# Moving six of nine group-norm tiles out of the end of a bidirectional recurrence into its last chunks

## The chip, the cores and the metric

The kernel runs on one core of one Trainium2 chip. The metric is the device time of one execution in microseconds. Its engines are TensorE (PE; weight loads are listed apart as PEld), VectorE (DVE), ScalarE (ACT), GpSimd (POOL) and SyncE (SP, which only issues DMAs here). ACT and POOL have DMA queues of their own.

## The reference, cut to what matters

The model has two layers of a first block and then a second block. Each layer of the first block projects 1040 tokens (16 meta tokens and 1024 real ones), runs a linear recurrence over the tokens in both directions, runs an attention (MLA) over the same tokens, mixes the two results with an output matrix, and goes through a mixture of experts. This case touches what follows the recurrence, the group norm of its output:

```python
y = y_f + y_b                       # forward and backward scan, (L, 8 heads, 64)
mu = jnp.mean(y, -1, keepdims=True)
var = jnp.mean(jnp.square(y - mu), -1, keepdims=True)
yn = ((y - mu) * lax.rsqrt(var + RWKV_GN_EPS)).reshape(B, L, RW) * gn_g + gn_b
out = (yn + (bonus_f + bonus_b).reshape(B, L, RW)) * g
```

It is elementwise over a row of 512 values, apart from one mean and one variance in each group of 64.

## The kernel before, in words

`recur` runs the scan in 17 chunks: chunk 0 holds the meta tokens forward, chunk c the 64 tokens from 16 + 64(c-1); the backward direction runs the same 17 chunks from the end. Both directions share each instruction, in the two halves of the 128 partitions. For chunk c the steps stand in the code in this order: `state` (PE products with the carried state S, then an ACT copy `Rs`), `solve` (PE product with an inverse `t64`, two ACT copies into `uv`), `next` (PE `dS`, then one DVE operation that updates S, L968), `out` (PE `Yp`, an ACT copy `ys`, two stores to `d_y` from POOL's queue, L978 and L981), and `bkt` for the chunk that follows (PE transposes and two ACT copies, L858).

The inverses are made ahead, for four chunks at a time, by `r_inv`: a DVE transpose, 31 pairs of small DVE multiplications and additions (`tm`, L876, and `Tn`, L877), and two more transposes (`TF`, `TT`). `turn` deals them out between the chunk's steps by a planned time: 2.2 us ahead of the S update, 0.8 us behind it, 5.2 us at the chunk's end, and all that is left at the end of every fourth chunk. `r_solve` turns `TT` into the `t64` of the next four chunks (copies on ACT, L893, and on POOL, L894, then PE and ACT). `r_prep`, which makes the DVE's masked products, looks eight chunks ahead, so chunks from 9 on have none of it.

`tc.manual_schedule` fixes the order of PE, ACT, DVE and SP in the loop to that of the code; each engine works its list in order. POOL's order, and everything behind the loop, is put in order by a planner at build time.

`r_post` does the group norm for one tile of up to 128 rows, nine tiles a layer, all called behind the loop. Its tiles come from a pool with two buffers, so a third tile waits for the first one's rows to be stored. A tile needs both directions of its rows, so tile 4 (rows 400 to 527) is complete after chunk 9, then 5, 3, 6, 2, 7, 1 one chunk apart, and 8 and 0 after chunk 16.

Behind `recur` in the code comes `mla`, which doesn't need the group norms; its weights are split into two parts by ACT and DVE (`split`, L251 and L252), then PE makes the products, and per block of tokens PE scores, a DVE maximum (L1151), ACT exponentials (L1155), PE transposes, and ACT and DVE copies and splits (L1166, L1169, L1170). The group norms' rows are first read in `mix_out`, behind the attention.

Of the kernel before, what the change touches and what calls it, by code (L numbers as in the profile page):

```python
# [10 lines left out]
F32 = mybir.dt.float32  # L11
# [5 lines left out]
ALU = mybir.AluOpType  # L17
# [155 lines left out]
class K:  # L173
# [521 lines left out]
    def recur(self, li, S):  # L695
        nc, tc, I = self.nc, self.tc, self.I
        with ExitStack() as es:
            LAG, GRP, N = 8, 4, 17

            def pool(name, bufs, **k):  # L700
                return es.enter_context(self.tpool(name=name, bufs=bufs, **k))

            ep = pool("r_e", 1)
            R = dict(li=li, S=S)
            R["dc"] = ep.tile([128, 32, 32], F32, name="dc")
            R["mask"] = []
            for d in range(2):
                m = ep.tile([128, 128], F32, name=f"cmask{d}")
                nc.sync.dma_start(m, self.C[f"cmask{d}"])
                R["mask"].append(m)  # L710
            bp, cp, mp = pool("r_b", 1), pool("r_c", 1), pool("r_m", 18)

            ap = pool("r_ar", 3)
            R.update(ap=ap, bp=bp, mp=mp, st=pool("r_s", 2), tp=pool("r_t", 2), qp=pool("q_t", 2, side="right"),
                     psa=pool("r_psa", 2, space=PSUM), psr=pool("r_psr", 2, space=PSUM),
                     psq=pool("r_psq", 2, space=PSUM), psc=pool("r_psc", 2, space=PSUM))
            R["t64"] = [cp.tile([128, 8 * GRP, 64], F32, name=f"t64{i}") for i in range(2)]
            for t in R["t64"] + [R["dc"]]:
                nc.gpsimd.memset(t, 0.0)

            R["pend"] = cp.tile([128, 8, N], F32, name="pend2")
            for d in range(2):
                for h in range(2):
                    nc.sync.dma_start(R["pend"][64 * d:64 * d + 64].rearrange("p (f h) c -> p f h c", h=2)[:, :, h],
                                      S["pend"][64 * h:64 * h + 64, d])
            R["St"] = [cp.tile([128, RW], F32, name=f"S{i}") for i in range(2)]
            qc = pool("q_c", 1, side="right")
            R["gb"] = self.bcast(qc, I["rwkv_gn_g"][li], RW, "gn_g")
            R["bb"] = self.bcast(qc, I["rwkv_gn_b"][li], RW, "gn_b")
            A = {}  # L730
            ET = mybir.EngineType
            with tc.manual_schedule(engines={ET.PE, ET.Activation, ET.DVE, ET.SP}):
                def turn(inv, left, us):

                    left += us
                    while left > 0:
                        w = next(inv, None)
                        if w is None:
                            return 0.0
                        left -= w  # L740
                    return left

                for s in range(GRP):
                    A[s] = self.r_prep(R, s)
                    for half in A[s]["halves"]:
                        half()
                    A[s]["diag"]()
                inv = self.r_inv(R, [A[c] for c in range(GRP)], 0)
                left = turn(inv, 0.0, 2.0)
                for s in range(GRP, LAG):  # L750
                    A[s] = self.r_prep(R, s)
                    if s == GRP:
                        V = self.r_load(R, 0)
                    for half in A[s]["halves"]:
                        half()
                        left = turn(inv, left, 3.5)
                    A[s]["diag"]()
                V["bkt"]()
                left = turn(inv, 0.0, 99.0)
                late = self.r_solve(R, [A[c] for c in range(GRP)], 0)  # L760
                next(late), next(late)
                C = self.r_chain(R, 0, A[0], V)
                C["own"]()
                for c in range(N):
                    g = c // GRP + 1
                    hs = [A[x] for x in range(GRP * g, min(N, GRP * g + GRP))]
                    if c % GRP == 0:
                        inv = self.r_inv(R, hs, g) if hs else iter(())
                        left = turn(inv, 0.0, 0.5)
                    P = None  # L770
                    if c + LAG < N:
                        P = A[c + LAG] = self.r_prep(R, c + LAG)
                    Vn = self.r_load(R, c + 1) if c + 1 < N else None
                    C["state"]()
                    next(late, None)
                    C["solve"]()
                    if P:
                        P["halves"][0]()
                    left = turn(inv, left, 2.2)
                    C["keep"]()  # L780
                    if Vn:
                        Cn = self.r_chain(R, c + 1, A[c + 1], Vn)
                        Cn["own"]()
                    C["next"]()
                    left = turn(inv, left, 0.8)
                    if P:
                        P["halves"][1]()
                    C["out"]()
                    next(late, None)
                    if P:  # L790
                        P["diag"]()
                    left = turn(inv, left, 99.0 if c % GRP == GRP - 1 else 5.2)
                    if Vn:
                        Vn["bkt"]()
                    if c % GRP == GRP - 1 and hs:
                        late = self.r_solve(R, hs, g)
                        next(late)
                    del A[c]
                    if Vn:
                        C = Cn  # L800
            for i in range(9):
                self.r_post(R, i)

    def r_fetch(self, pool, names, S, ch):

# [179 lines left out]
    def r_post(self, R, i):  # L985

        nc, tp, S, li = self.nc, R["qp"], R["S"], R["li"]
        gb, bb = R["gb"], R["bb"]
        c0, n = TT[i]
        y0 = tp.tile([128, RW], F32, name="q_y0")  # L990
        y1 = tp.tile([128, RW], F32, name="q_y1")
        v = tp.tile([128, RW], F32, name="q_v")
        g = tp.tile([128, RW], F32, name="q_g")
        for t, src in ((y0, S["y"][0]), (y1, S["y"][1]), (v, S["v"][0]), (g, S["g"])):
            (nc.gpsimd if t in (y0, y1) else nc.sync).dma_start(t[:n], src[c0:c0 + n, :])
        nc.gpsimd.tensor_tensor(y0[:n], y0[:n], y1[:n], ALU.add)
        yv = y0[:n].rearrange("p (h v) -> p h v", h=8)
        y1v = y1[:n].rearrange("p (h v) -> p h v", h=8)
        vv = v[:n].rearrange("p (h v) -> p h v", h=8)
        mu = tp.tile([128, 8], F32, name="q_mu")  # L1000
        nc.vector.tensor_reduce(mu[:n], yv, AX.X, ALU.add)
        nc.vector.tensor_scalar(mu[:n], mu[:n], 1.0 / 64, None, ALU.mult)
        nc.gpsimd.tensor_tensor(yv, yv, mu[:n, :, None].to_broadcast([n, 8, 64]), ALU.subtract)
        nc.scalar.activation(y1[:n], y0[:n], AF.Square)
        vr = tp.tile([128, 8], F32, name="q_vr")
        nc.vector.tensor_reduce(vr[:n], y1v, AX.X, ALU.add)
        nc.scalar.activation(vr[:n], vr[:n], AF.Sqrt, scale=1.0 / 64, bias=self.eps["gn"][:n])
        nc.vector.reciprocal(vr[:n], vr[:n])
        nc.gpsimd.tensor_tensor(vv, vv, S["bonus"][:n, i, :, None].to_broadcast([n, 8, 64]), ALU.mult)
        nc.gpsimd.tensor_tensor(v[:n], v[:n], bb[:n], ALU.add)  # L1010
        nc.vector.tensor_tensor(yv, yv, vr[:n, :, None].to_broadcast([n, 8, 64]), ALU.mult)
        nc.vector.tensor_tensor(y0[:n], y0[:n], gb[:n], ALU.mult)
        nc.vector.tensor_tensor(y0[:n], y0[:n], v[:n], ALU.add)
        nc.gpsimd.tensor_tensor(y0[:n], y0[:n], g[:n], ALU.mult)
        nc.scalar.dma_start(S["yr"][c0:c0 + n, :], y0[:n])
        if self.dbg:
            self.dbg(f"yr{li}", (T, RW), y0[:n], lambda a: a[c0:c0 + n])

# [1504 lines left out]
```

## Time and profile before

| | |
|---|---|
| three runs | 4386.04, 4390.46, 4396.25 us, median 4390.46 |
| the profiled execution | 4402.54 us, span 4400.7 us |
| busy share of the span | PE 87%, PEld 72%, DVE 63%, ACT 42%, POOL 22% |
| layer 1: last seven S updates to the end of its recurrence | 618.86 us to 679.04 us |
| layer 1: attention | 679.04 us to about 992 us |
| the same in layer 2 | 2187.08 us to 2247.75 us, and on to about 2551 us |

All times in a trace count from the start of the span. The busy share is an average over stages that have different limits: in the recurrence PE, ACT and DVE hand work to each other chunk by chunk, in the attention PE has most of the work. So what the change moves is read from the two stretches that it touches, once in each layer.

### The profile page before, as it was taken

How to read it: one execution, taken by the hardware profiler on the slowest of the kernel's cores; microseconds unless marked ns; L12 is line 12 of the kernel's file. 1: busy time of each engine (PE TensorE's matmuls, PEld its weight loads, DVE VectorE, ACT ScalarE, POOL GpSimd, SP SyncE). 2: the span in 40 equal slices, each digit the busy share in tenths (PEclk: the TensorE clock that was granted, in tenths of full speed). 3: DMA queues.
4: the chain of work that ended last, by engine and by line, in shares of the span. 5: the costliest groups of instructions: out<-in, count | busy, mean ns of one | idle time of the engine just before them, and what ended most of it. 6: DMA issues, size and time to landing. Idle time of an engine off the chain costs nothing. (4 is left out here: it accounts for less than half of the span.)

```text
span 4400.7 us, 68329 instructions
## 1 busy us (share of the span) xinstructions
PE 3830.7 (87%) x27155; PEld 3157.1 (72%) x27155; DVE 2767.7 (63%) x4684; ACT 1869.7 (42%) x3033; POOL 988.2 (22%) x719
## 2 busy tenths in 40 slices
PE   7888897899699688897887896997898889999998
PEld 7677676786576476776776775765786677888786
DVE  7763777757698757627668577997644753333354
ACT  4323445542387543233555532876424522111232
POOL 2331124201242243311233012331422410000000
PEclk9788798999799887886988997999998899999999
DMA  4446663113499833447641043998521121111232
GB/s 154 101 129 183 160 161 108 37 54 128 160 345 346 300 102 101 115 143 172 165 125 58 1 172 131 340 335 309 181 73 29 53 97 58 48 48 43 90 126 81
DMA packets 384153, 611.94 MB, mean 139 GB/s; under 512 B 50467, under 2 KB 217602, under 8 KB 381762
## 3 DMA queue, kind: packets, MB, share of 16 engines
q1 hardware_dynamic: 278402, 485.38, 35.3%
q10 hardware_dynamic: 85200, 70.97, 5.4%
q0 software_dynamic: 20224, 51.15, 3.7%
q8 instruction: 216, 3.54, 0.3%
q14 instruction: 111, 0.91, 0.1%
HBM read 491.65 MB, written 123.45 MB: 140 GB/s over the span
## 5 line engine op out<-in xcount | busy, mean ns | idle before, releaser
L252 DVE TENSOR_TENSOR w13l<-xw,w13h 128x1024 fp32r<-128x1024 f32 x248 | 296.4, 1220 | 57.5 <-ACT w13h L251 53.9
L251 ACT ACTIVATE w13h<-xw 128x1024 fp32r<-128x1024 f32 x256 | 267.4, 1058 | 130.3 <-PE x_hp L258 76.6
L256 PE MATMUL pp_ps<-T_hi,pw_hi 128*128 128x348 f32 x912 | 309.7, 340 | 8.7 <-ACT T_hi L1752 2.9
L257 PE MATMUL pp_ps<-T_lo,pw_hi 128*128 128x348 f32 x912 | 305.4, 335 | 1.4 <-DVE T_lo L1757 1.3
L258 PE MATMUL pp_ps<-T_hi,pw_lo 128*128 128x348 f32 x912 | 304.3, 334 | 0.0
L2414 PE MATMUL f_mm<-F_hi,f_wh 128*128 128x512 f32 x704 | 222.8, 398 | 1.7 <-ACT F_hi L251 1.7
L2414 PE MATMUL f_mm<-F_lo,f_wh 128*128 128x512 f32 x704 | 222.6, 397 | 0.0
L2414 PE MATMUL f_mm<-F_hi,f_wl 128*128 128x512 f32 x704 | 222.3, 397 | 0.0
L256 PE MATMUL x_hp<-w13h,x_h 128*96 128x512 f32 x512 | 208.5, 407 | 0.1
L257 PE MATMUL x_hp<-w13l,x_h 128*96 128x512 f32 x512 | 204.7, 400 | 0.0
L258 PE MATMUL x_hp<-w13h,x_l 128*96 128x512 f32 x512 | 204.0, 398 | 0.0
L256 PEld LDWEIGHTS pp_ps<-T_hi,pw_hi 128*128 128x128 f32 x912 | 179.8, 197 | 21.8 <-issue 7.8
L257 PEld LDWEIGHTS pp_ps<-T_lo,pw_hi 128*128 128x128 f32 x912 | 179.8, 197 | 5.1 <-DVE T_lo L1757 2.6
L287 POOL TENSOR_TENSOR g_x<-g_x,g2g 128x1024 f32<-128x1024 f32 x6 | 14.3, 2385 | 750.4 <-ACT g_x L284 750.4
L258 PEld LDWEIGHTS pp_ps<-T_hi,pw_lo 128*128 128x128 f32 x912 | 179.5, 197 | 3.0 <-issue 3.0
L252 DVE TENSOR_TENSOR f_wl<-F_raw,f_wh 128x1024 fp32r<-128x1024 f32 x44 | 53.7, 1221 | 203.2 <-ACT f_wh L251 203.2
L251 ACT ACTIVATE f_wh<-F_raw 128x1024 fp32r<-128x1024 f32 x44 | 46.4, 1060 | 307.0 <-PE f_mm L2414 301.4
L1616 POOL DMA_INDIRECT d_y<-x_o,r_idx x64 | 102.8, 1606 | 312.1 <-DVE x_al L252 288.8
L825 PE MATMUL aa<-ar_p,bk_p 64*128 64x128 f32 x1088 | 134.0, 376 | 40.2 <-DVE A L827 33.6
L2414 PEld LDWEIGHTS f_mm<-F_hi,f_wh 128*128 128x128 f32 x704 | 133.1, 189 | 34.4 <-ACT F_hi L251 2.0
L2414 PEld LDWEIGHTS f_mm<-F_lo,f_wh 128*128 128x128 f32 x704 | 132.7, 189 | 32.8 <-DVE F_lo L252 0.6
L2414 PEld LDWEIGHTS f_mm<-F_hi,f_wl 128*128 128x128 f32 x704 | 132.9, 189 | 32.4
(630 smaller groups left out, 11221.3 us busy)
## 6 DMA issues: line engine op xcount, KB each, us to landing
xw<-in_moe_w SPq DMA_DIRECT2D x256, 512.0 KB
xw<-in_moe_w SPq DMA_DIRECT2D x64, 1024.0 KB
wd_raw<-in_w_down SPq DMA_DIRECT2D x44, 512.0 KB
pw_raw<-in_w_in SPq DMA_DIRECT2D x36, 512.0 KB
d_AR<-AR ACTq DMA_DIRECT2D x32, 544.0 KB
d_BK<-BK ACTq DMA_DIRECT2D x32, 544.0 KB
ar_p<-d_AR SPq DMA_DIRECT2D x68, 256.0 KB
bk_p<-d_BK SPq DMA_DIRECT2D x68, 256.0 KB
```

The source lines that it names most:

```text
L251: nc.scalar.activation(hi, src, AF.Copy)
L252: (lo_eng or nc.vector).tensor_tensor(lo, src, hi.bitcast(F32), ALU.subtract)
L256: mm(out, wh, xh, start=first, stop=False)
L257: mm(out, wh, xl, start=False, stop=False)
L258: mm(out, wl, xh, start=False, stop=last)
L287: e1.tensor_tensor(out[:n], out[:n], gb[:n], ALU.mult)
L825: nc.tensor.matmul(aa[d][:, h - z], bk[q, h], ar[q, h], start=True, stop=True)
L1616: nc.gpsimd.indirect_dma_start(out=y2[:, :], out_offset=bass.IndirectOffsetOnAxis(ap=si, axis=0), in_=y, in_offset=None, bounds_check=2 * ...
L2414: nc.tensor.matmul(p[:, j], a[:, k], b[:, k, 512 * j:512 * j + 512], start=st, stop=sp)
```

## The change

`r_post` becomes a generator with four steps, and six of the nine tiles (4, 5, 3, 6, 2, 7) are started in chunks 10 to 15, one a chunk, behind `out`. Every half chunk each open tile is taken one step on: `norms` is called behind `out`, and behind the last `turn` ahead of the next chunk's `bkt`. The steps are: (1) the loads (y0 and y1 from POOL's queue, v and g from SP's) and two POOL operations on v; (2) the sum of both directions, now on DVE where it was on POOL, the sum over the group and its scaling on DVE, and the subtraction on POOL; (3) the square on ACT and its sum on DVE; (4) the root on ACT, and the rest. The finished rows are stored from POOL's queue where it was ACT's. Tiles 1, 8 and 0 run behind the loop as before, in that order.

```diff
+                order, rows = [4, 5, 3, 6, 2, 7, 1, 8, 0], []
+                rest = [self.r_post(R, i) for i in order]
+
+                def norms(c, new=False):
+                    if new and 10 <= c < 16:
+                        rows.append(rest.pop(0))
+                    for r in list(rows):
+                        if next(r, 0) == 0:
+                            rows.remove(r)
                 for c in range(N):
...
                     C["out"]()
+                    norms(c, True)
                     next(late, None)
                     if P:
                         P["diag"]()
                     left = turn(inv, left, 99.0 if c % GRP == GRP - 1 else 5.2)
+                    norms(c)
                     if Vn:
                         Vn["bkt"]()
...
-            for i in range(9):
-                self.r_post(R, i)
+            for r in rows + rest:
+                for _ in r:
+                    pass
...
-        nc.gpsimd.tensor_tensor(y0[:n], y0[:n], y1[:n], ALU.add)
...
+        vr = tp.tile([128, 8], F32, name="q_vr")
+        nc.gpsimd.tensor_tensor(vv, vv, S["bonus"][:n, i, :, None].to_broadcast([n, 8, 64]), ALU.mult)
+        nc.gpsimd.tensor_tensor(v[:n], v[:n], bb[:n], ALU.add)
+        yield
+        nc.vector.tensor_tensor(y0[:n], y0[:n], y1[:n], ALU.add)
         nc.vector.tensor_reduce(mu[:n], yv, AX.X, ALU.add)
         nc.vector.tensor_scalar(mu[:n], mu[:n], 1.0 / 64, None, ALU.mult)
         nc.gpsimd.tensor_tensor(yv, yv, mu[:n, :, None].to_broadcast([n, 8, 64]), ALU.subtract)
+        yield
         nc.scalar.activation(y1[:n], y0[:n], AF.Square)
-        vr = tp.tile([128, 8], F32, name="q_vr")
         nc.vector.tensor_reduce(vr[:n], y1v, AX.X, ALU.add)
+        yield
         nc.scalar.activation(vr[:n], vr[:n], AF.Sqrt, scale=1.0 / 64, bias=self.eps["gn"][:n])
         nc.vector.reciprocal(vr[:n], vr[:n])
-        nc.gpsimd.tensor_tensor(vv, vv, S["bonus"][:n, i, :, None].to_broadcast([n, 8, 64]), ALU.mult)
-        nc.gpsimd.tensor_tensor(v[:n], v[:n], bb[:n], ALU.add)
...
         nc.gpsimd.tensor_tensor(y0[:n], y0[:n], g[:n], ALU.mult)
-        nc.scalar.dma_start(S["yr"][c0:c0 + n, :], y0[:n])
+        nc.gpsimd.dma_start(S["yr"][c0:c0 + n, :], y0[:n])
```

## Rows read from the trace of the kernel before

**Rows 1.** Attention by windows: us, busy us of each engine (instructions), PE clock, DMA share.

```profile
726.00:826.00 100.00, 79.47 (x441) 71.81 (x441) 83.76 (x152) 64.09 (x130) 48.74 (x42) 0.81 0.26 74
826.00:926.00 100.00, 88.29 (x575) 79.90 (x576) 59.89 (x132) 53.81 (x131) 0.00 (x0) 0.95 0.00 1
...
2289.00:2390.00 101.00, 74.44 (x446) 66.52 (x447) 85.49 (x156) 64.96 (x133) 51.68 (x42) 0.88 0.24 72
2390.00:2490.00 100.00, 88.49 (x585) 79.50 (x584) 59.06 (x131) 53.43 (x130) 0.00 (x0) 0.97 0.01 3
```

**Rows 2.** ACT in the first of these windows, grouped by line: count, busy, mean ns.

```profile
L1007 ACT ACT_TABLE_LOAD x7 | 9.0, 1283 | 0.8 <-POOL q_y L1014 0.7
L1004 ACT ACTIVATE q_y<-q_y 128x512 f32<-128x512 f32 x7 | 4.4, 623 | 4.4 <-POOL q_y L1003 4.4
```

**Rows 3.** Recurrence by windows, S update to S update, chunks 10 to 15.

```profile
618.86:629.00 10.14, 10.14 (x282) 8.66 (x277) 9.52 (x23) 5.06 (x9) 2.02 (x4) 1.00 0.76 195
629.00:641.84 12.84, 10.59 (x244) 8.38 (x238) 3.41 (x8) 6.24 (x9) 5.13 (x8) 0.73 0.42 115
641.84:651.84 10.00, 10.00 (x340) 8.81 (x336) 8.27 (x23) 5.71 (x10) 2.02 (x4) 1.00 0.57 143
651.84:660.40 8.56, 8.56 (x236) 7.38 (x230) 7.97 (x19) 3.41 (x6) 2.02 (x4) 1.00 0.71 185
660.40:670.53 10.13, 9.64 (x250) 8.11 (x246) 9.51 (x22) 5.06 (x9) 1.97 (x4) 1.00 0.59 181
...
2219.77:2228.33 8.56, 8.56 (x236) 7.38 (x230) 7.98 (x20) 3.41 (x6) 2.02 (x4) 1.00 0.64 164
```

**Rows 4.** DVE in order of time; in brackets the idle time before, and its releaser.

```profile
641.84 0.69 DVE L968 TENSOR_TENSOR S<-dS,pend 128x512 f32<-128x512 f32 x1 [8.28 <-PE dS L966]
...
651.84 0.69 DVE L968 TENSOR_TENSOR S<-dS,pend 128x512 f32<-128x512 f32 x1 [1.01 <-PE dS L966]
...
660.40 0.68 DVE L968 TENSOR_TENSOR S<-dS,pend 128x512 f32<-128x512 f32 x1
...
670.53 0.65 DVE L968 TENSOR_TENSOR S<-dS,pend 128x512 f32<-128x512 f32 x1
```

**Rows 5.** Instructions on tile q_y, both layers: min/median/max ns, first and last start.

```profile
L1001 DVE TENSOR_REDUCE q_mu<-q_y x18: 662/668/686, 693.8 to 2378.4; 128x8 f32<-128x512 f32 x16, 16x8 f32<-16x512 f32 x2
L1003 POOL TENSOR_TENSOR q_y<-q_y,q_mu x18: 1032/1049/1690, 695.9 to 2379.8; 128x512 f32<-128x512 f32 x16, 16x512 f32<-16x512 f32 x2
...
L1011 DVE TENSOR_TENSOR q_y<-q_y,q_vr x18: 669/675/2590, 703.8 to 2385.4; 128x512 f32<-128x512 f32 x16, 16x512 f32<-16x512 f32 x2
...
L1014 POOL TENSOR_TENSOR q_y<-q_y,q_g x18: 1257/1284/3252, 709.1 to 2387.6; 128x512 f32<-128x512 f32 x16, 16x512 f32<-16x512 f32 x2
```

**Rows 6.** The reciprocal's line, and POOL's two operations on v by form.

```profile
L1008 DVE RECIPROCAL q_vr<-q_vr x18: 179/192/206, 702.5 to 2385.1; 128x8 f32<-128x8 f32 x16, 16x8 f32<-16x8 f32 x2
...
L1010 POOL TENSOR_TENSOR q_v<-q_v,gn_b 128x512 f32<-128x512 f32 x7 | 9.4, 1340 | 0.4
L1009 POOL TENSOR_TENSOR q_v<-q_v,s_bonus 128x512 f32<-128x512 f32 x7 | 8.9, 1269 | 3.5 <-DMA q_v<-d_v 3.5
```

**Rows 7.** POOL and DVE in order of time, in the attention and in the recurrence.

```profile
705.08 2.82 POOL L1135 TENSOR_TENSOR qpe<-qpe,qr 128x1040 f32<-128x1040 f32 x1 [1.64 <-DVE q_vr L1008]
...
705.86 2.59 DVE L1011 TENSOR_TENSOR q_y<-q_y,q_vr 128x512 f32<-128x512 f32 x1
...
715.36 6.93 DVE L1099 TENSOR_TENSOR qs<-qpe,qs 64x1040 fp32r<-64x1040 f32 x1
```

**Rows 8.** ACT in order of time, ends of chunks 11, 15 and 16.

```profile
627.50 1.08 ACT L858 ACTIVATE bkt<-tps 128x512 f32<-128x512 f32 x2
629.17 2.12 ACT L893 ACTIVATE t<-TT 32x1024 f32<-32x1024 f32 x2 [0.58 <-DVE TT L883]
...
670.70 0.84 ACT L893 ACTIVATE t<-TT 32x256 f32<-32x256 f32 x2 [0.54 <-DVE TT L883]
...
679.04 2.03 ACT L251 ACTIVATE cqh<-cq_raw 128x1040 fp32r<-128x1040 f32 x2
```

**Rows 9.** POOL's queue in order of time: a load behind a store, and its user.

```profile
492.54 0.51 POOL L995 DMA_DIRECT2D q_y<-d_y  x1 [2.75 <-DMA d_y<-ys]
...
690.60 3.27 POOL L996 TENSOR_TENSOR q_y<-q_y,q_y 16x512 f32<-16x512 f32 x2 [3.63 <-DMA q_y<-d_y]
```

## The prediction

> **What bounds the kernel now.** I read the page first for the engines' shares, then cut the two stretches that the change touches into windows, and then read DVE, ACT and POOL there in order of time.
>
> The stretch that gives work away is the start of each layer's attention. Four windows show it [rows 1]. In layer 1 the 100 us from 726 hold 441 matmuls, the next 100 us hold 575, of the same kind; in layer 2 it is 446 in 101 us against 585 in 100. The difference in the windows is the group norms: POOL is busy 48.74 us in the first and not at all in the second, DVE 83.76 against 59.89, ACT 64.09 against 53.81. ACT's part has seven squares, so seven of the nine tiles lie in this window, and seven extra table loads of 1.28 us for the root, each of which the exponential then has to undo [rows 2].
>
> The stretch that takes the work is the recurrence from chunk 10. The windows from S update to S update [rows 3] show that DVE has almost no room there: busy 9.52 of 10.14 us, 3.41 of 12.84, 8.27 of 10.00, 7.97 of 8.56 and 9.51 of 10.13. What is missing in the second is one wait of 8.28 us, where PE and ACT make the next inverses; in the third it is a wait of 1.01 us; ahead of the S updates at 660.40 and 670.53 there is no idle time at all [rows 4]. There the S update, on which the next chunk hangs, is queued behind the inverses' small operations: DVE is already the engine that ends last. PE is as full in the same windows, but it has no work added. Layer 2's window of the same chunk is alike to 0.01 us [rows 3].
>
> **The gain in the attention.** At the pace of the undisturbed window the 441 matmuls take 441/575 × 100 = 76.7 us, so seven tiles cost 23.3 us, and in layer 2 446/585 × 100 = 76.2 of 101, so 24.8 us. That is 3.4 us a tile. Three tiles stay behind the loop. Before, two tiles ran ahead of the window, so I let one of the three fall into it: 23.3 + 24.8 − 2 × 3.4 = 41.3 us for both layers. The lower bound is six ninths of 48.1, or 32 us. The upper bound adds the start: there one DVE split lasts 6.93 us [rows 7], and were that and the three tiles gone too it would be 48.1 + 2 × 6.9 = 62 us. I don't count it, since tiles 1, 8 and 0 will put the same POOL operations there. The store moved from ACT's queue to POOL's is in these numbers: ACT no longer waits at its issue for POOL's last multiplication.
>
> **The cost in the recurrence, DVE's own work.** A tile has six DVE operations over 128x512 at about 0.67 us each (the sum of both directions, which comes over from POOL, two reductions, and three in step 4) and two over 128x8, for which I take the reciprocal's 0.19 [rows 5, 6]: 6 × 0.67 + 2 × 0.19 = 4.4 us; step 2 alone is 0.67 + 0.67 + 0.19 = 1.5. From chunk 11 on every chunk has all the steps of one tile's worth, step 3 and 4 of the older and 2 of the newer.
>
> **POOL's work beside it.** A tile keeps four POOL operations: 1.27 and 1.34 us on v [rows 6], 1.05 for the subtraction and 1.28 for the last product [rows 5], 4.9 together. In the trace a DVE operation with two operands from SBUF doesn't run beside one of these: the product that usually takes 0.67 us took 2.59 when it started at 705.86, with POOL at work from 705.08 to 707.90, and it ended 0.55 us behind POOL [rows 5, 7]. The inverses' operations are of the same kind, with a broadcast operand like that one, but no row shows one beside a reading POOL operation. So the price for a tile lies between 0 and 4.9 us. I take 4.0: the nearest row shows full blocking, and a part of POOL's time will meet S updates, reductions and transposes.
>
> The Trainium skill says of this, in "SBUF — State Buffer", section "SBUF: two separate sides", that VectorE and GpSimd share one pair of ports, held for a whole instruction, and that a DVE operation with two SBUF inputs takes part in it against a GpSimd operation that reads SBUF. By that rule the price would be the whole 4.9 us a tile, and the sum below about 6 us more; by the other bound, no blocking, the sum would be near zero. The 2.59 us row agrees with the rule.
>
> **ACT's order.** Step 4's root stands ahead of the `bkt` copies, and those ahead of the `t64` copies that open the solve for the next four chunks. The root needs step 3's reduction, which stands on DVE behind the S update. At the end of chunk 11 the `bkt` copies ran at 627.50, ahead of the S update at 629.00, and `t64` at 629.17 [rows 3, 8]. After: S update to 629.69, reduction 0.67, root 0.3 with about 0.3 of handing over, `bkt` 1.08, so `t64` at about 631.9, 2.7 us later. This waits on PE and ACT, in the window where DVE idles 8.28 us, so DVE's own work is hidden there and only the 2.7 counts. At the end of chunk 15 `t64` ran at 670.70; after, 2.6 us later by the same steps. At the end of chunk 16 tile 7's square (0.62), reduction (0.67), root (0.3) and their handing over (0.3) stand ahead of the attention's first split at 679.04: 1.9 us.
>
> **Sum for one layer**, from S update to S update:
> - chunk 10 to 11: step 2 of the first tile 1.5, POOL beside it (two operations on v, one subtraction, of 3.7) 2.5: 4.0
> - 11 to 12: 2.7
> - 12 to 13: 4.4 + 4.0, less the 1.0 of idle time: 7.4
> - 13 to 14, and 14 to 15: 8.4 each
> - behind 15: 2.6 and 1.9
>
> That is 35.4 us a layer, 70.8 for both. Without blocking it is 1.5 + 2.7 + 3.4 + 4.4 + 4.4 + 4.5 = 20.9 a layer, 41.8 for both; with all of it (3.7 in chunk 10, 4.9 in the three others) 39.3, or 78.6.
>
> **What is moved past which queue.** SP gets two loads a tile, behind the `uv` loads of the next chunk and ahead of the `ar` loads of the one after, which the code issues a chunk ahead of their use; a wait of a few us there is hidden by that. POOL gets the loads and the store. A `d_y` load went out 2.75 us after the store before it had landed, with the stores of sixteen chunks still to come, so it waits only for its own rows [rows 9], and those are a chunk old. The third tile's load waits for the first one's store, issued half a chunk before: about 1 us is left over for it with chunks of 17 us, and the load then has some 10 us until step 2, by what stands between on DVE (0.8 + 5.2 us of inverses, 3 us of the older tile, and POOL's share). So I cost these at nothing; the cover is the lengthened chunk.
>
> **Net:** 70.8 − 41.3 = +29.5 us. The profiled execution took 4402.5 us and would take 4432; the median of the runs is 12.1 us lower, so 4390.5 + 29.5 = 4420 us.
>
> **The rivals.**
> - *DVE and POOL don't block each other in the recurrence.* For it: no row shows an inverse's operation blocked. Against: the row of 2.59 us. Then 41.8 − 41.3 = +0.5 us: 4391, no change that a measurement tells.
> - *The chunk is set by PE and ACT, and DVE's added work hides.* For it: PE is busy for the whole of the window from 651.84 [rows 3]. Then only ACT's order counts, 2.7 + 2.6 + 1.9 = 7.2 us a layer, and 14.4 − 41.3 = −27 us: 4363, faster. It decides from the point where a chunk's DVE work, 8.0 + 8.4 us, stays under the chain's length; the chain would have to be 16 us, and the shortest chunk is 8.56. That speaks against it, but a larger gain in the attention (62 us) together with no blocking gives the same side, 4370.
> - *The steps wait for their data.* A load was used 3.63 us after POOL was free [rows 9], and if POOL's queue, stuck on a store's landing, makes step 2 late by 3 us in six chunks of both layers, 36 us come on top: 4456. Against it stand the 10 us of room above.
>
> The skill's same page and section warns that a DVE operation in a two-port mode keeps GpSimd from writing the descriptors of its DMAs. This would make the third rival likelier; the inverses' operations have two inputs and are not of that mode, and no row shows such an issue held up.
>
> **How the numbers follow.** The forecast has 0.52; no blocking 0.20; DVE hidden or the larger gain 0.20; waits for data 0.08. What a measurement can tell here is 0.2%, or 8.8 us. The forecast and the waits are slower by more (0.60); of the no-blocking case, which lies at +0.5 with 10 us to either side, I give 0.16 to no change, 0.03 to faster and 0.01 to slower. So faster 0.23, same 0.16, slower 0.61. The forecast alone runs from 4403 (half of POOL's time blocked: 60 us for both layers, and the attention 3 us a layer better, so 60 − 47 = +13) to 4437 (78.6 − 32 = +46.6). The range for 8 in 10 goes down to 4374, into the faster cases, and up to 4438.
>
> **What would show it.** Right: chunks 12 to 15 last 15 to 18 us each from S update to S update, with DVE busy or blocked for all of it; inverses' operations of 0.4 us stretched to more than 1 us beside POOL; the first 100 us of attention behind the first exponential with 540 matmuls or more and one or two pairs of table loads. Wrong: chunks of 9 to 12 us, or idle time ahead of DVE's sum in step 2 released by a DMA, or an attention that starts as slowly as before.

## The result

| | runs | median, us | lowest to highest |
|---|---|---|---|
| before | 4 | 4390.04 | 4386.04 to 4396.25 |
| after | 4 | 4421.50 | 4410.77 to 4428.80 |

The ratio is 1.0065, with a 95% interval of 1.0045 to 1.0085: slower by 20 to 37 us, forecast +29.5. The profiled execution of after took 4410.77 us and is the fastest of its four; that of before, 4402.54, is slower than all its timed ones. So I compare the two traces stretch by stretch, and totals by ratios of medians. The two executions themselves are only 8.1 us apart, since the part between layer 1's attention and layer 2's chunk 9, which the change doesn't touch, took 1186 us in that of before and 1170 in that of after. The other traces lie between, but for e12, which changes chunks 4 and 8. Stretches in us, in each cell layer 1 / layer 2, "chunk 9" meaning its S update (610.30 us in layer 1 of before; the 618.86 us in the table of before is the first of the last six updates, not seven), "split" the first `cql`, "exp" the attention's first exponential, "end" the last write of `y_att`:

| run | chunk 9 to 15 | 15 to last `ys` | `ys` to split | split to exp | exp to end |
|---|---|---|---|---|---|
| before | 60.2 / 60.0 | 7.9 / 8.7 | 1.7 / 1.7 | 46.3 / 40.7 | 265.9 / 261.9 |
| after | 85.7 / 85.5 | 10.5 / 11.6 | 14.6 / 13.1 | 41.2 / 39.5 | 240.6 / 241.4 |
| e1, all behind, sum on VectorE | 58.4 / 59.2 | 9.0 / 7.9 | 1.7 / 1.7 | 41.9 / 45.6 | 267.3 / 268.9 |
| e5, all behind, sum on GpSimd | 57.7 / 59.6 | 8.7 / 8.4 | 1.7 / 1.7 | 43.1 / 43.2 | 262.4 / 259.8 |
| e2, no GpSimd operations | 77.0 / 79.1 | 10.6 / 22.8 | 16.1 / 5.7 | 42.8 / 42.2 | 239.2 / 236.6 |
| e3, splits first | 85.8 / 86.6 | 11.6 / 10.4 | 12.9 / 14.4 | 42.3 / 40.9 | 237.6 / 242.0 |
| e7, splits fixed | 86.0 / 86.0 | 11.6 / 10.6 | 13.4 / 14.1 | 42.0 / 41.3 | 239.2 / 237.7 |
| e4, store from ScalarE | 108.8 / 109.3 | 20.3 / 21.2 | 5.8 / 5.8 | 46.0 / 46.8 | 233.4 / 234.1 |
| e6, after, sum on GpSimd | 91.4 / 92.4 | 10.9 / 13.6 | 5.3 / 17.5 | 52.0 / 43.7 | 234.7 / 236.6 |
| e8, four tiles spread | 78.9 / 79.4 | 11.4 / 11.7 | 9.3 / 9.2 | 46.8 / 42.6 | 246.6 / 243.7 |
| e9, order 8, 0, 1 | 86.0 / 85.0 | 10.6 / 11.6 | 4.7 / 4.7 | 44.7 / 42.9 | 237.7 / 236.7 |
| e10, pace in chunk 12 | 83.8 / 82.1 | 12.8 / 26.8 | 16.4 / 5.8 | 46.0 / 47.2 | 231.0 / 242.3 |
| e11, one tile | 64.9 / 65.5 | 11.5 / 10.6 | 1.7 / 1.7 | 40.4 / 48.3 | 258.0 / 259.1 |
| e12, pace, all behind | 58.5 / 61.2 | 10.6 / 9.6 | 1.7 / 1.7 | 42.1 / 38.7 | 260.1 / 260.3 |

In the windows of after (us, busy us and count of PE, PEld, DVE, ACT, POOL, then PE clock, DMA share, GB/s), three windows from S update to S update answer to [rows 3] (chunks 13 to 15, a chunk being named by the update at its end), then comes the end of chunk 16, and the attention's windows answer to [rows 1]:

```profile
642.73:659.00 16.27, 12.35 (x372) 10.67 (x366) 15.38 (x31) 7.98 (x14) 8.42 (x11) 1.00 0.61 170
659.00:675.57 16.57, 8.11 (x204) 6.82 (x204) 15.81 (x28) 4.17 (x8) 8.65 (x11) 0.90 0.66 176
675.57:691.41 15.84, 12.32 (x236) 10.10 (x236) 15.05 (x31) 4.17 (x8) 8.65 (x11) 0.68 0.62 159
...
701.93:716.54 14.61, 0.00 (x0) 0.00 (x0) 4.76 (x9) 3.99 (x6) 4.54 (x6) 0.50 0.87 289
...
757.69:857.69 100.00, 89.63 (x572) 81.56 (x573) 60.48 (x137) 53.73 (x132) 1.79 (x2) 0.93 0.00 1
857.69:957.69 100.00, 88.46 (x587) 78.10 (x587) 59.96 (x137) 51.70 (x131) 0.00 (x0) 0.97 0.00 1
2318.17:2418.17 100.00, 89.50 (x576) 81.36 (x577) 61.15 (x138) 54.37 (x133) 1.80 (x2) 0.95 0.01 1
```

Chunks 13 to 15 last 15.8 to 16.6 us, with DVE busy for 95% of them and PE for 8 to 12 us of 16. The attention's first 100 us hold 572 and 576 matmuls where they held 441 and 446: it starts at its undisturbed pace. PE's granted clock in these windows moved with it, from 0.81 and 0.88 [rows 1] to 0.93 and 0.95; what share of the gain is the clock's no run separates. The new hole is the window from 701.93: 14.61 us without one matmul, all engines mostly idle. After in order of time, at two places (start, us, engine, line; in brackets the idle time before and its releaser):

```profile
642.73 0.69 DVE L981 TENSOR_TENSOR S<-dS,pend 128x512 f32<-128x512 f32 x1 [6.24 <-PE dS L979]
...
656.20 2.44 DVE L889 TENSOR_TENSOR tm<-Z,Tn 128x247 f32<-128x247 f32 x1
...
656.30 1.06 POOL L1020 TENSOR_TENSOR q_y<-q_y,q_mu 128x512 f32<-128x512 f32 x1
...
657.31 1.04 POOL L1014 TENSOR_TENSOR q_v<-q_v,s_bonus 128x512 f32<-128x512 f32 x1
...
659.00 0.68 DVE L981 TENSOR_TENSOR S<-dS,pend 128x512 f32<-128x512 f32 x1
...
705.19 2.03 ACT L251 ACTIVATE cqh<-cq_raw 128x1040 fp32r<-128x1040 f32 x2 [0.95 <-DMA cq_raw<-d_cq]
706.30 0.58 POOL L1008 DMA_DIRECT2D q_y<-d_y  x1 [3.50 <-DMA d_yr<-q_y]
707.07 0.55 POOL L994 DMA_DIRECT2D d_y<-ys  x1 [0.19 <-issue]
...
708.12 0.57 POOL L1008 DMA_DIRECT2D q_y<-d_y  x1
...
712.43 0.69 DVE L1017 TENSOR_TENSOR q_y<-q_y,q_y 128x512 f32<-128x512 f32 x1 [8.53 <-DMA q_y<-d_y]
...
716.10 0.63 ACT L1022 ACTIVATE q_y<-q_y 128x512 f32<-128x512 f32 x1 [8.89 <-POOL q_y L1020]
716.54 1.23 DVE L252 TENSOR_TENSOR cql<-cq_raw,cqh 128x1040 fp32r<-128x1040 f32 x1
```

The upper half shows that of the 8.28 us of idle time ahead of chunk 12's update [rows 4] 6.24 are left, with none ahead of chunk 13's, and an inverse operation of 0.41 us lasting 2.44 beside two POOL operations. In both layers every inverse operation of over 1 us in chunks 13 to 15 ends 0.1 to 0.3 us behind one of POOL's on a tile. Against the same operations in before, the inverses' rows in these three chunks are 7.7 and 7.2 us longer. The lower half shows tile 1, the first behind the loop: its load waits on POOL's queue for the store of tile 2, whose buffer it takes (3.50 us), chunk 16's own rows go out behind it, and DVE stands for 8.53 us in front of tile 1's sum with tile 7's last steps and the split of `cq` queued behind. ACT is held in the same way by the tile's square.

### The profile page after: what moved, and what is told of

Its sections match the earlier page's. It is cut to its first block, busy times and chain, and to the rows that moved or that the text cites. A ratio compares the mean times of both kernels' runs of the same rounds, so it can differ in the third digit from the quotient of the medians.

```text
span 4408.8 us, 68296 instructions
## 1 busy us (share of the span) xinstructions
PE 3806.8 (86%) x27155; PEld 3140.5 (71%) x27155; DVE 2775.2 (63%) x4702; ACT 1834.8 (42%) x3005; POOL 977.8 (22%) x719
## 4 chain that ended last, share of the span: by engine, by line
PE 37%; DVE 5%; DMA 3%; ACT 2%; issue 2%; POOL 1%; SPq 0%; DVEq 0%; ACTq 0%; POOLq 0%
PE f_mm L2430 11%; PE a_ft L2002 3%; DMA xw<-in_moe_w 2%; PE g_mm L256 2%; PE g_mm L258 2%; PE g_mm L257 2%; PE ms L1165 2%; PE x_hp L256 1%; PE x_hp L257 1%; PE x_hp L258 1%; PE o_mm L256 1%; PE o_mm L257 1%; PE o_mm L258 1%; PE u_mm L258 1%; PE d_s L2205 1%
## 5 line engine op out<-in xcount | busy, mean ns | idle before, releaser
L1632 POOL DMA_INDIRECT d_y<-x_o,r_idx x64 | 112.2, 1753 | 311.3 <-DVE x_al L252 295.2
```

What stands on the lines that cost most here:

```text
L1632: nc.gpsimd.indirect_dma_start(out=y2[:, :], out_offset=bass.IndirectOffsetOnAxis(ap=si, axis=0), in_=y, in_offset=None, bounds_check=2 * ...
```

## The experiments

Times "by the ratio" are (ratio − 1) × 4390 us against the kernel before. By that after stands at +28.5.

**e1, the move undone.** Line numbers in the traces are those of each kernel.

```diff
-                order, rows = [4, 5, 3, 6, 2, 7, 1, 8, 0], []
+                order, rows = list(range(9)), []
...
-                    if new and 10 <= c < 16:
+                    if new and False:
```

> The changed kernel with the move undone: all nine tiles stand behind the loop, in the order 0 to 8; the sum on VectorE, the early operations on v and the store from GpSimd's queue stay. If the move makes the difference (gain in attention, cost in the recurrence), layer 1 goes back to 60 us from the S update of chunk 9 to that of chunk 15 and to 46 + 265 us from the first split of cq to the last write of y_att, and the time is that of the kernel before, 4390 us (4382 to 4398). If instead the sum on VectorE, which waits for loaded rows, is what holds the splits at the end of chunk 16, the 11 to 13 us there stay in each layer although no tile is in the loop, and the time is 4410 to 4415 us.

Measured: 4406.97 us, ratio 1.0044 (1.0026 to 1.0063), +19 us. Both expectations missed. The recurrence and the end of chunk 16 are back to before's, yet the time is not: two thirds of the loss stay with what was left of the change in the kernel.

**e5, the sum back on GpSimd as well.**

```diff
-        nc.vector.tensor_tensor(y0[:n], y0[:n], y1[:n], ALU.add)
+        nc.gpsimd.tensor_tensor(y0[:n], y0[:n], y1[:n], ALU.add)
```

> The kernel of the run before with all nine tiles behind the loop (4407 us), and the sum of the two directions back on GpSimd; the early operations on v and the store from GpSimd's queue stay. If the sum costs VectorE its own 0.7 to 1.2 us a tile in the attention's bound stretch too, 18 tiles of it are the 19 us, and the time goes back to 4388 us (4380 to 4396). If the early operations or the store on GpSimd's queue are what costs, it stays at 4400 to 4410 us.

Measured: 4381.86 us, ratio 0.9982 (0.9968 to 0.9996), the fastest version, 8 us under before by the ratio. The one line is worth 27 us with nine tiles behind the loop, 1.5 us for each of 18 tiles. The first 100 us of the attention, layer 1 and 2, for e1 and then for e5:

```profile
722.71:822.71 100.00, 76.84 (x430) 69.11 (x431) 77.56 (x153) 61.45 (x126) 42.61 (x43) 0.83 0.25 76
2287.10:2387.10 100.00, 77.51 (x451) 67.48 (x452) 79.25 (x157) 62.77 (x131) 40.93 (x37) 0.84 0.22 66
```

```profile
720.09:820.09 100.00, 79.74 (x469) 70.90 (x470) 82.89 (x157) 63.95 (x136) 53.09 (x48) 0.88 0.24 73
2278.47:2378.47 100.00, 79.80 (x481) 71.36 (x482) 83.94 (x159) 64.33 (x136) 56.09 (x49) 0.87 0.24 73
```

With the sum on DVE 430 and 451 matmuls, without it 469 and 481. DVE is not the fuller for it: it is less busy in e1 (77.56 against 82.89 us). So the sum's own 0.67 us is not the whole story; how the planner orders DVE and ACT around it must take part, and I have not separated the two.

**e2, GpSimd's four operations left out** in the six tiles of the loop; the three others keep them.

```diff
+        pool = i in (8, 1, 0)
+        if pool:
             nc.gpsimd.tensor_tensor(vv, vv, S["bonus"][:n, i, :, None].to_broadcast([n, 8, 64]), ALU.mult)
```

> The changed kernel without GpSimd's four operations (bonus product, gn_b, mean subtraction, product with g) in the six tiles of the loop, which are so not normalised fully; everything else stands. If GpSimd's operations beside VectorE's cost what VectorE's row of 2.44 us and the like show (3.5 us a tile), chunks 12 to 15 lose some 3 us each against the changed kernel: the 25.5 us that S update 9 to S update 15 has over the kernel before falls to 10 to 15 us in each layer and the time to about 4397 us (4390 to 4403). If VectorE's own 4.4 us a tile are the whole cost, the recurrence keeps 22 to 25 us and the time stays at 4414 to 4422 us. The 11 to 13 us behind chunk 16 stay in either case.

Measured: 4400.11 us, ratio 1.0029 (1.0014 to 1.0044), 16 us under after by the ratio. Chunks 13 to 15 of this kernel:

```profile
642.43:656.13 13.70, 12.07 (x372) 10.54 (x366) 12.33 (x32) 7.76 (x14) 3.67 (x7) 1.00 0.40 114
656.13:668.96 12.83, 9.21 (x204) 8.05 (x204) 12.10 (x29) 3.57 (x8) 3.73 (x7) 0.87 0.85 217
668.96:683.30 14.34, 9.39 (x205) 7.96 (x204) 13.62 (x30) 3.87 (x8) 3.83 (x8) 0.88 0.89 247
```

They take 40.87 us, after 48.68, before 28.70 [rows 3]. So of a tile's price in these chunks (40.87 − 28.70) / 3 = 4.1 us is DVE's own, and (48.68 − 40.87) / 3 = 2.6 us is POOL beside it, which is what the stretched rows of after add up to (7.7 and 7.2 us for three tiles); in e2 no row of the inverses is stretched. Layer 2 gives 3.7 and 2.6 us. The time came out as expected; chunk 9 to 15 fell less far than I wrote, 17 and 19 us above before and not 10 to 15, since chunk 12 didn't get shorter. The wait at tile 1's sum is longer here, 13.6 and 13.7 us where after has 8.5 and 7.0. In layer 2 the planner put that tile's square on ACT ahead of the last `ys`, so the wait counts in the column ahead of it (22.8 us).

**e3, the three tiles written down behind the attention's first splits.**

```diff
-            for r in rows + rest:
-                for _ in r:
-                    pass
+            S["rest"] = rows + rest
...
                 self.split(kph, kpl, kp)
+            for r in S["rest"]:
+                for _ in r:
+                    pass
```

> The changed kernel with the three tiles behind the loop (1, 8, 0) written down after the attention's first splits and not ahead of them. If the wait of tile 1 for its buffer and its rows is what holds cq's split, the stretch from the last copy of ys to the split of cq falls from 14.6 and 13.1 us to 2 to 4 us in the two layers, the recurrence keeps its 25.5 us, and the time is about 4400 us (4394 to 4408). If the projections wait for something else (the load of cq_raw, GpSimd's queue), or the attention gives it back because the three tiles come later, the time stays at 4415 to 4424 us.

Measured: 4415.73 us, ratio 1.0058 (1.0040 to 1.0076); the hole is 12.9 and 14.4 us. The planner puts tile 1's sum ahead of the split all the same, so this tested the order of writing, not the wait.

**e7, the same with the splits in program order** on ScalarE and VectorE.

```diff
+                with self.tc.manual_schedule(engines={ET.Activation, ET.DVE}):
+                    for f in range(2):
+                        self.split(cqh[:, f], cql[:, f], cq[:, f])
```

> The run with the splits written down first left VectorE's order to the planner, which still put tile 1's sum ahead of the split of cq. Here the splits stand in program order on ScalarE and VectorE, ahead of the three tiles. If that order is the cost, the stretch from the last ys to cq's split falls to 3 to 5 us in both layers, the projections begin 9 to 11 us earlier, and the time is 4398 to 4406 us. If the attention gives it back, because three tiles' work falls later into it, the stretch from the first split to the last write of y_att grows by as much and the time stays at 4412 to 4420 us.

Measured: 4415.05 us, ratio 1.0056 (1.0034 to 1.0079); hole 13.4 and 14.1 us. The order holds among the splits only; the sum still comes ahead of them.

**e9, tile 1 last.**

```diff
-                order, rows = [4, 5, 3, 6, 2, 7, 1, 8, 0], []
+                order, rows = [4, 5, 3, 6, 2, 7, 8, 0, 1], []
```

> The changed kernel with the three tiles behind the loop in the order 8, 0, 1 and not 1, 8, 0. Tiles 8 and 0 need chunk 16's rows, so the planner can't count on their sum before cq's split. If VectorE's wait at tile 1's sum is what holds the splits, the stretch from the last ys to cq's split falls from 14.6 and 13.1 us to 2 to 5 us, the recurrence keeps its 25.5 us, and the time is 4396 to 4408 us. If the splits wait for the late load of cq_raw, they stay 10 us or more behind ys, and the time is 4415 to 4424 us.

Measured: 4397.76 us, ratio 1.0009 (0.9995 to 1.0023): 24.6 us under after by the ratio, no difference from before that can be measured. The end of chunk 16 in e9:

```profile
705.83 2.01 ACT L251 ACTIVATE cqh<-cq_raw 128x1040 fp32r<-128x1040 f32 x2
705.96 0.20 DVE L1026 RECIPROCAL q_vr<-q_vr 128x8 f32<-128x8 f32 x1 [0.37 <-ACT q_vr L1025]
...
707.72 0.69 DVE L1029 TENSOR_TENSOR q_y<-q_y,q_v 128x512 f32<-128x512 f32 x1
...
708.33 1.23 DVE L252 TENSOR_TENSOR cql<-cq_raw,cqh 128x1040 fp32r<-128x1040 f32 x1
```

The hole is 4.71 us in both layers, and the split follows tile 7's last addition without a wait. That settles that the wait for tile 1's rows was the hole, but for some 3 us a layer over before that tile 7's last steps take, and that the late load of `cq_raw` was not.

**e6, after with the sum back on GpSimd** (the diff of e5).

> The changed kernel with the sum back on GpSimd, its six tiles still in the loop. If VectorE's wait for tile 1's rows, at the sum, is what holds the splits behind chunk 16, the 14.6 and 13.1 us there fall to 2 to 4 us, and VectorE has 0.7 us less of its own in each tile: recurrence 20 to 24 us over the kernel before instead of 25.5, time 4390 to 4400 us. If GpSimd's sum blocks VectorE as much as it spares it, the recurrence keeps its 25 us or gets up to 6 us longer, and if the splits wait for something other than the sum, the 11 to 13 us stay as well: 4415 to 4425 us.

Measured: 4438.70 us, ratio 1.0109 (1.0083 to 1.0134), 19 us over after by the ratio and above both expectations. In the loop the trade turns round: chunk 9 to 15 grows by 5.7 and 6.9 us. In layer 1, where DVE has nothing of tile 1 ahead of the split, the hole falls to 5.3 us. In layer 2 it grows to 17.5, with tile 1's rows again at its root, this time through POOL:

```profile
2296.62 0.56 POOL L1008 DMA_DIRECT2D q_y<-d_y  x1 [4.74 <-DMA d_yr<-q_y]
...
2302.26 1.25 POOL L1017 TENSOR_TENSOR q_y<-q_y,q_y 128x512 f32<-128x512 f32 x1 [5.08 <-DMA q_y<-d_y]
...
2303.54 0.69 DVE L1018 TENSOR_REDUCE q_mu<-q_y 128x8 f32<-128x512 f32 x1 [16.09 <-POOL q_y L1017]
```

**e4, the finished rows stored from ScalarE's queue.**

```diff
-        nc.gpsimd.dma_start(S["yr"][c0:c0 + n, :], y0[:n])
+        nc.scalar.dma_start(S["yr"][c0:c0 + n, :], y0[:n])
```

> The changed kernel with each finished row stored from ScalarE's queue, as in the kernel before. If a store that waits for GpSimd's product holds ScalarE's copies of uv and ys in the loop, each of the six tiles costs 1 to 4 us more in the recurrence, and the time is 4430 to 4460 us. If GpSimd's queue is what the stores burden (chunk 16's rows and tile 1's load stand behind them), the end of chunk 16 gets 2 to 4 us shorter in each layer and the time falls to 4413 to 4418 us. If neither, 4421 us.

Measured: 4461.93 us, ratio 1.0167 (1.0137 to 1.0196). ACT in one chunk of e4:

```profile
658.78 0.30 ACT L1025 ACTIVATE q_vr<-q_vr,eps_gn 128x8 f32<-128x8 f32 x1
667.68 0.36 ACTq L1031 DMA_DIRECT2D d_yr<-q_y  x1
668.09 1.08 ACT L871 ACTIVATE bkt<-tps 128x512 f32<-128x512 f32 x2 [9.01 <-POOL q_y L1030]
669.06 0.61 ACT L958 ACTIVATE Rs<-Rp 128x512 f32<-128x512 f32 x1
```

ACT stands at the store until POOL's product is there, 9.01 us, with the chain's copies behind it, and chunks 13 to 15 take 20.3 to 20.5 us each. Of the change's parts that were undone in the loop the move of the store is the dearest to miss: 45 us by the ratio, the sum on VectorE 19 (e6).

**e8, four tiles spread.** The sum is on GpSimd and v's operations come behind it; the core of the edit:

```diff
+                plan = {(10, "out"): (0,), (10, "end"): (0,), (11, "out"): (1,), (11, "end"): (1,), (11, "late"): (0, 1),
+                        (12, "late"): (0, 1), (12, "uv"): (0,), (12, "next"): (1,),
+                        (14, "out"): (2,), (14, "end"): (3,), (15, "out"): (2,), (15, "end"): (3,), (15, "late"): (2, 3),
+                        (16, "late"): (2, 3), (16, "uv"): (2,), (16, "out"): (3,)}
...
-                    left = turn(inv, left, 2.2)
+                    left = turn(inv, left, 6.0 if c == 12 else 2.2)
```

> Four tiles only in the loop, with the sum on GpSimd, and their VectorE steps where the kernel before leaves VectorE idle: tiles 4 and 5 in the 8.3 us ahead of the S update of chunk 12, tiles 3 and 6 behind that of chunk 15; the inverse gets 3.8 us more of its work in chunk 12's turn. Five tiles stay behind the loop. If VectorE's time in chunks 12 to 15 is what the change lost, chunk 9 to chunk 15 takes 60 to 64 us, the attention gains 3.4 us a tile, 13 to 14 us a layer, and the time is 4362 to 4380 us, under both kernels. If GpSimd's operations or ScalarE's roots hold the chain in those two stretches as well, each costs 3 to 6 us and the time is 4380 to 4395 us.

Measured: 4416.48 us, ratio 1.0054 (1.0038 to 1.0070), above both expectations. The place "late" comes twice in chunks 11 and 15, so the steps ran about half a chunk earlier than the expectation says. Chunk 12's update came 24.8 and 24.3 us behind chunk 11's:

```profile
626.77 2.12 ACT L912 ACTIVATE t<-TT 32x1024 f32<-32x1024 f32 x2 [1.08 <-DVE TT L902]
...
628.12 1.27 POOL L1023 TENSOR_TENSOR q_v<-q_v,gn_b 128x512 f32<-128x512 f32 x1
...
629.35 1.04 POOL L1027 TENSOR_TENSOR q_y<-q_y,q_mu 128x512 f32<-128x512 f32 x1
...
630.96 1.26 POOL L1021 TENSOR_TENSOR q_y<-q_y,q_y 128x512 f32<-128x512 f32 x1 [0.58 <-DMA q_y<-d_y]
...
632.17 2.12 POOL L913 COPY t<-TT 32x1024 f32<-32x1024 f32 x2
...
636.67 0.63 ACT L1029 ACTIVATE q_y<-q_y 128x512 f32<-128x512 f32 x1 [5.62 <-POOL q_y L1027]
637.33 0.60 ACT L964 ACTIVATE Rs<-Rp 128x512 f32<-128x512 f32 x1
637.82 1.18 ACT L932 ACTIVATE t<-O 32x512 f32<-32x512 f32 x2
```

POOL makes its half of the `t64` copies 5.4 us after ACT's half, because three of the tiles' operations stand ahead, one of them waiting for rows. That delays the second tile's subtraction on POOL in turn, and the wait that ends last is ACT's: it stands 5.62 us (5.34 in layer 2) at that tile's square, with the chain's `Rs` and `t` queued behind, and the solve's products start only with that `t`, at 638.54. So the second case happened, POOL's and ACT's steps hold the chain, at a higher price than expected.

**e11, one tile**, on e5: tile 4 loaded in chunk 10, its steps in chunk 12.

```diff
+                    if c == 12:
+                        for us in (2.0, 0.8, 0.0):
+                            next(rest[0], None)
+                            left = turn(inv, left, us)
```

> Built on the fastest kernel so far (all tiles behind the loop, sum on GpSimd, 4382 us): tile 4 alone goes into chunk 12, where VectorE is idle ahead of the S update, its rows loaded two chunks earlier, its steps behind the copies of uv, with 2.8 us more of the inverse between them. If an idle VectorE is all that a tile in the loop needs, chunk 9 to chunk 15 stays at 57 to 60 us, the attention gains 3.4 us a layer, and the time is 4370 to 4378 us. If GpSimd's operations hold the chain there, chunk 11 to 12 grows by 3 to 6 us and the time is 4380 to 4390 us.

Measured: 4393.13 us, ratio 1.0010 (0.9998 to 1.0022): 12 us over e5 by the ratio. Chunk 9 to 15 grew by 7.2 and 6.0 us, chunk 12 by 3.5 and 4.0 of it, as in the second case, though the time is over its 4390. In chunks 10, 11 and 13, where the code has nothing of the tile but its loads, POOL's operations on it stretch the inverses' rows by 6.5 us in either layer. In chunk 12 of layer 1 DVE waits 1.53 us for the tile's square, which stands on ACT behind the copies of `uv`, and the S update is queued behind the tile's last steps. An idle DVE was not all that a tile needs.

**e10, after with one number of the pace changed.**

```diff
-                    left = turn(inv, left, 2.2)
+                    left = turn(inv, left, 9.0 if c == 12 else 2.2)
```

> The changed kernel with one number changed: in chunk 12 the inverse may hand out 9.0 us of its steps ahead of the S update, and not 2.2, so that VectorE's idle 6.2 us ahead of that update take work out of chunks 13 to 15. If VectorE is what bounds chunks 12 to 15, S update 12 to S update 15 falls from 48.7 us to 42 to 44 us in both layers, S update 11 to 12 grows by at most 2 us, and the time is 4409 to 4414 us. If ScalarE's or GpSimd's steps of the tiles bound them, the stretch stays at 47 to 49 us and the time at 4418 to 4424 us.

Measured: 4427.23 us, ratio 1.0079 (1.0062 to 1.0096). Chunks 12 to 15 of e10:

```profile
629.16:650.14 20.98, 13.37 (x368) 11.84 (x368) 19.48 (x36) 9.92 (x16) 13.51 (x19) 0.84 0.61 165
650.14:665.35 15.21, 10.19 (x268) 8.97 (x268) 14.42 (x28) 5.57 (x10) 4.82 (x5) 0.84 0.34 91
665.35:682.14 16.79, 9.83 (x204) 8.65 (x204) 15.90 (x31) 4.28 (x8) 9.32 (x13) 0.80 0.71 190
682.14:690.96 8.82, 8.10 (x173) 7.03 (x175) 7.05 (x11) 3.05 (x6) 7.89 (x11) 0.68 0.83 204
```

Chunks 13 to 15 fall by 7.9 us to 40.8, more than expected: work taken off VectorE there shortens them, as it does where an engine is the bound. But chunk 12 grows by 6.0, not by 2, and the time lies above both expectations. The idle 6.24 us had let POOL's operations run at no cost. With the inverse in their place its rows in chunk 12 are stretched by 4.8 us in layer 1 and 3.9 in layer 2, where after has none stretched, and most of the gain is paid back: 1.9 us (3.3 in layer 2) are left of it from chunk 9 to 15. The end took them: the wait at tile 1's sum is 14.9 and 14.8 us here, 8.5 and 7.0 in after; why it grew isn't shown. In layer 2 it lies ahead of the last `ys`, as in e2, and is the 26.8 us of the table:

```profile
2285.57 0.69 DVE L1017 TENSOR_TENSOR q_y<-q_y,q_y 128x512 f32<-128x512 f32 x1 [14.75 <-DMA q_y<-d_y]
...
2288.34 0.63 ACT L1022 ACTIVATE q_y<-q_y 128x512 f32<-128x512 f32 x1 [16.27 <-POOL q_y L1020]
2288.99 0.60 ACT L987 ACTIVATE ys<-Yp 128x512 f32<-128x512 f32 x1
```

**e12, the same pace on e5**, in chunks 4, 8 and 12.

```diff
-                    left = turn(inv, left, 2.2)
+                    left = turn(inv, left, 9.0 if c and c % GRP == 0 else 2.2)
```

> The fastest kernel so far (all nine tiles behind the loop, sum on GpSimd, 4382 us) with the inverse allowed 9.0 us of its steps ahead of the S update in chunks 4, 8 and 12, where its profile shows VectorE busy for 5.9, 5.9 and 3.4 us of 19.9, 16.9 and 10.2 us. If VectorE also bounds the three chunks that follow each of these, as it does in the changed kernel, chunk 13 to 15 falls from 28.8 us to about 26 us, the other groups' by as much, and the time is 4364 to 4376 us. If the chain through TensorE and ScalarE sets these chunks, the stretches stay and the time is 4378 to 4386 us; if the steps ahead hold the S updates of chunks 4, 8 and 12, those stretches grow by 2 to 6 us each and it is 4385 to 4400 us.

Measured: 4410.08 us, ratio 1.0048 (1.0032 to 1.0064), the third case, and more than it allows. Chunks 13 to 15 gained 1.1 and 1.2 us; chunks 4 and 8 lost 4.0 to 8.7 and chunk 12 2.4 and 3.4. DVE in chunk 8 of e12:

```profile
590.52 1.96 DVE L883 STREAM_TRANSPOSE Z<-dc 128x1024 f32<-128x1024 f32 x1 [2.64 <-ACT dc L846]
601.49 1.29 DVE L840 TENSOR_TENSOR A<-aa,cmask 128x512 f32<-128x512 f32 x2 [9.02 <-PE aa L838]
602.70 0.20 DVE L889 TENSOR_TENSOR tm<-Z,Tn 128x31 f32<-128x31 f32 x1
...
611.10 0.68 DVE L981 TENSOR_TENSOR S<-dS,pend 128x512 f32<-128x512 f32 x1
```

The idle 9.02 us lie ahead of the mask product, and the inverse is queued behind that; so the 8.4 us of steps came into the way of the S update and not into the idle time.

## Why the prediction was right

The time lies 1.5 us from the forecast. The mechanism in the loop was right, DVE as the bound with POOL's operations beside it, but that the number fits so closely is luck: the end of chunk 16 was put 20 us too low, and that error cancelled against two of 11 us, the loop's cost put too high and the attention's gain too low. From the two traces, both layers:

| term | forecast | measured | 
|---|---|---|
| chunk 9 to 15 | +61.8 | +51.0 |
| 15 to the last `ys` | +5.2 | +5.6 |
| end of chunk 16 | +3.8 | +24.2 |
| attention, from the split | −41.3 | −52.1 |
| sum | +29.5 | +28.7 |

- **DVE bounds the loop's last chunks: right for 13 to 15.** They last 15.8 to 16.6 us with DVE busy for 95%, and e10 shortens them by taking DVE's work out. Chunk 12, of 15.0 and 15.3 us, still has some 7 us of idle DVE, as the forecast's 2.7 us for it assumes. The rival in which DVE's work hides behind PE and ACT is out. By chunks of layer 1, from 9 to 10 on, the growth is 1.7, 1.7, 2.2, 6.3, 8.0 and 5.7 us where the forecast had 0, 4.0, 2.7, 7.4, 8.4 and 8.4; the first is POOL's work on tile 4's v, at 611.88 and 613.16, which the planner put ahead of chunk 10's update.
- **DVE's own 4.4 us a tile: 4.1** by e2 (3.7 in layer 2).
- **POOL beside DVE, taken at 4.0 of 4.9: 2.6** by e2 and by the stretched rows. The two bounds were right and the choice too high. With 2.6 for 4.0, and 2.0 for the 2.5 of the first chunk, the forecast's own sum for chunk 9 to 15 is 52 us where 51.0 were measured, so this is the term that made it 61.8. The rule that the Trainium skill states in "SBUF — State Buffer", section "SBUF: two separate sides", that a DVE operation with two SBUF inputs takes part in the lock against a reading GpSimd operation, is borne out as far as that it happens, by the 2.44 us row; the whole of POOL's time as a price is not. (By the forecast's own working that whole time would have added 78.6 − 70.8 = 7.8 us, not the 6 it states.) Leaving POOL out takes 16 of the 28.5 us away, so the rival without blocking is out.
- **The end of chunk 16 at 1.9 us a layer: wrong.** It took 12.9 and 11.3. The step that failed is "So I cost these at nothing; the cover is the lengthened chunk", on the load that waits for an earlier tile's store. The row it leaned on [rows 9] says that POOL's queue stood idle for 2.75 us until the landing of a store let the load go, so it showed such a wait in small. The step held for the six tiles of the loop (DVE's idle time ahead of the sums has one wait for a load in a layer, 8.5 and 7.0 us, and that is tile 1's), but the first tile behind the loop has no long chunk to cover it, and the planner put its sum ahead of the split. This was my third rival, at a place where I hadn't looked; e9 takes it away and gives 24.6 us back by the ratio, 18.2 of them in the hole itself by the two traces. The sign that I had named for it, idle time ahead of DVE's sum released by a DMA, is there.
- **The attention's gain, 41.3: 52.1**, inside its bounds of 32 to 62. Behind the first exponential it is 45.8 us, ahead of it 6.3, where the forecast had nothing. The step that was mis-sized is "I let one of the three fall into it": none does. The last root of a group norm (L1025) is at 753.89 and 2314.4 us, the first exponential at 757.69 and 2318.2, and no table load follows it, where before had seven roots a layer behind it. So all seven tiles have left that stretch, at 45.8 / 14 = 3.3 us a tile, about the forecast's 3.4. From e1, with the sum on DVE in both, it is 26.7 and 27.5 us for seven tiles, 3.9 a tile.
- **Where the sum stands was taken as part of DVE's 4.4 us and no more.** By e1 and e5 that is worth 27 us with all tiles behind the loop; with the tiles in the loop the same exchange costs 19 us the other way (e6). The move itself, from e1 to e9, both with the sum on VectorE and neither with the wait for tile 1's rows, is a gain of 15 us by the ratios (1.0044 to 1.0009), 5 to 26 by their intervals taken as independent.

So with the sum on VectorE the move of six tiles is not what loses. Tile 1's place behind the loop costs 24.6 us. From e5, the sum on VectorE costs 27 us while all tiles stand behind the loop, and the move gives 15 of them back, so e9 stays 12 us behind e5. The only version that is faster than before leaves all tiles behind the loop: e5, by 2 to 14 us. How much of that is due to the early operations on v and how much to the store on GpSimd's queue was not tried, nor was the sum on VectorE for the six tiles and on GpSimd for the other three.

## What to carry to other kernels

When a loop hands over to a stage that a planner orders, cost the first piece of work behind the loop by itself: what its buffer and its rows wait for, and what is queued behind it on each engine. Idle time of an engine is only room if the work put there stands in the queue at that place, and if every other engine that the work uses is free there too: e8, e11 and e12 each failed on one of these. Undo a change part by part even when its total came out as forecast, since here an error of 20 us had cancelled against two of 11.

## What the runs showed that I had not expected

- A 0.41 us operation of DVE lasted 2.44 us beside two POOL operations, 1.06 and 1.04, that followed each other directly, and ended 0.29 us behind the second.
- A load through DRAM behind a store was slow on both sides: 4.74 us of waiting for the store of the buffer's last tile, then 5.08 us until the rows were used (e6); in after 3.50 us (6.5 from the store's issue at 699.82 to the load's), and then 4.3 from the issue of the second load (708.12) to the sum (712.43).
- Executions of one kernel differ by a few tenths of a per cent, by and large with the mean granted clock: the 18 runs of before beside e1 went from 4378.0 us (clock 0.909) to 4403.0 (0.903). A single profile can't rank kernels that are this close.
